# Two layers of a pooling, attention and product-key expert trunk on one core: pick transposes queued later, first V tiles by token tile, eight modulation rows moved from the U pass to the V pass

## The chip, the cores and the metric

The kernel runs on one core of one Trainium2 chip. The metric is the device time of one execution in microseconds (us). The time before is 1764.51 us, the median of three runs (1763.54 to 1767.49).

## What is computed

There are two layers, 256 tokens and 1024 channels. Each layer is a modulated norm, a mixer (causal pooling and sliding-window attention) and a PEER block, each with a gated residual. The modulation of a layer is six rows of 1024 values (`sh1, sc1, g1, sh2, sc2, g2`), a product of the conditioning vector with a 1024 x 6144 matrix. The change lies in the PEER block, cut here to what matters:

```python
mod = cond @ w_ada[l] + b_ada[l]                 # sh1, sc1, g1, sh2, sc2, g2
h2 = rms_norm(x, norm2_g[l]) * (1.0 + sc2) + sh2
q = (h2 @ wq).reshape(T, 8, 2, 128)
s = einsum('thpd,pnd->thpn', q, subkeys)         # 16 score rows of 128 keys for a token
top_s, top_i = top_k(s, 16)                      # then the 16 best sums of each head:
best_s, best_j = top_k(cand, 16)                 # 128 experts of 16384 for a token
gate = softmax(best_s)
act = gelu(h2 @ u[expert]) * gate
x = x + g2 * (act @ v[expert])
```

## The kernel before, in words

**Dense instead of gathered.** The kernel doesn't gather experts. It multiplies all 16384 rows of U and all of V, with a gate that is zero where an expert was not picked. The weights are 128 tiles of U and 128 of V a layer, each 128 x 1024 float32 (512 KB).

**The load stream.** One list of items (`Stream`, built at lines 199 to 218) holds every weight tile in the order of its use. SP issues the loads (L82) into a pool of five buffers called raw. A U or V tile is then split into two half-precision parts: ACT makes the high part (L87) and VectorE (DVE) the low part (L88), in one of five buffers called hl. Only when DVE has read it is a raw buffer free for the next load. Between the weight tiles, `spread` puts background items: rows of the modulation matrix (eight items of 512 KB for one of the six rows) and, in layer 0, the ten tiles of the next layer's input matrix ("pre"). A background row is consumed by one DVE instruction (L291, or L289 for the first of eight) that adds into one accumulator, acc_a; after the eighth, TensorE (PE) reduces it (L265 for scales and shifts, L302 for gains), and only then may the next row begin to fill acc_a.

**The U pass** (`peer`, the loop over `ip_`): 64 pairs of U tiles, 48 matmuls each (L362), then a gelu on ACT (L903) into act. While the first 32 pairs run, a generator `picks` (68 steps, `NPICK`) does the top-16 work on DVE, a fixed number of steps after each pair. Its last steps, for each token tile `tt` of 128 tokens, compare and add (L806 to L820), and end with four PE transposes (L829) and an ACT copy into pk (L830). From pair 32 on, a generator `gates` takes one step a pair: DVE builds one-hot tiles (L845 to L851), 16 small matmuls (L855, L857) make the gate of eight tokens for 64 of the 128 expert tiles, and DVE multiplies it into act (L860). A first round of 32 steps covers expert tiles 0 to 63 and ends with the U pass; a second round covers 64 to 127 and ends with V tile 63.

**The V pass**: for each pair of V tiles ACT (L929) and DVE (L930) split 512 columns of act (two expert tiles, 256 tokens each) into high and low parts in hbuf, which until then held the normed input that the U matmuls read. Each V tile is 12 matmuls of 512 columns (L370), six for each token tile. The last five tiles run token tile by token tile (`tail`), so that the residual of the first can start early.

**What sets the order.** Every engine works through a queue in a fixed order, which a scheduler writes at build time from the order in the program. `tc.issue_after(x)` only puts instructions behind x in the queue of x's own engine; it adds no wait between engines.

Of the kernel before, what the change touches and what calls it, by code (L numbers as in the profile page):

```python
# [121 lines left out]
def trunk(ctx, tc, ins, out):  # L122
# [82 lines left out]
    for l in range(L):  # L205
        if l == 1:
            items += conv_items(ins["wout"][1], 8, None, "pre")
        items += conv_items(ins["wq"][l], 16, WS, "w")
        uu = conv_items(ins["u"][l], 128, WS, "u")
        vv = conv_items(ins["v"][l], 128, VS, "v")  # L210
        if l == 0:
            uu = spread(uu, ada_rows(1, SC1) + ada_rows(1, SH1) + ada_rows(1, SC2), 8, 126)
            pre = conv_items(ins["win"][1], 10, None, "pre")
            vv = spread(vv, ada_rows(0, G2) + ada_rows(1, G1) + ada_rows(1, SH2) + pre, 66, 126)
        else:
            vv = spread(vv, ada_rows(1, G2), 66, 126)
        items += uu + vv
        vend[l] = len(items) - 1
# [137 lines left out]
    def mm_u(pt, w, hi, lo):  # L356

        wh, wl = (a.rearrange("p (k c) -> p k c", k=8) for a in w)
        n = 0
        for k in range(8):  # L360
            for a, b in ((wh, hi), (wh, lo), (wl, hi)):
                pe.matmul(pt, lhsT=a[:, k], rhs=b[:, k], start=n == 0, stop=n == 23)  # L362
                n += 1

    def mm_v(acc, w, ahi, alo, first, end):
# [356 lines left out]
    def peer(l, q5):  # L722
# [16 lines left out]
        def picks():  # L739

            If = [a.f(256, F16).rearrange("p (j r) -> p j r", j=16) for _ in range(2)]
            cand = a.f(8 * 112).rearrange("p (h m) -> p h m", h=8)
            B = a.f(256).rearrange("p (h r) -> p h r", h=16)
            J = a.f(256, U16).rearrange("p (h r) -> p h r", h=16)
            gt = a.f(256).rearrange("p (h r) -> p h r", h=16)
            m, t1, t2, ja = (a.f(256) for _ in range(4))
            jh = [a.f(512, F16).rearrange("p (n t) -> p n t", t=2) for _ in range(2)]
            o1 = a.f(2048, F16).rearrange("p (h r j) -> p h r j", h=8, r=16)
            o2 = a.f(2048, F16).rearrange("p (h r j) -> p h r j", h=8, r=16)
            ip = a.f(512, F16).rearrange("p (t s n) -> p t s n", t=2, s=2)  # L750
            gsum = a.f(16)
            gp = [a.f(256, F16) for _ in range(2)]
            Ji = a.f(256, I32)
            for j4 in range(4):
                for tt in range(2):
                    for j in range(j4 * 4, j4 * 4 + 4):
                        top16(V[tt][:, j], I[tt][:, j], sc[tt][:, j], tmp[j % 2])
                        yield
            V2 = [v.rearrange("p (h s) r -> p h s r", s=2) for v in V]
            I2 = [i.rearrange("p (h s) r -> p h s r", s=2) for i in If]  # L760
            for tt in range(2):
                dve.tensor_copy(If[tt], I[tt])
                for n, (alo, an, bn, c0) in enumerate(((0, 4, 16, 0), (4, 12, 4, 64))):
                    dve.tensor_tensor(
                        out=cand[:, :, c0:c0 + an * bn].rearrange("p h (a b) -> p h a b", a=an),
                        in0=V2[tt][:, :, 0, alo:alo + an].unsqueeze(3).to_broadcast([P, 8, an, bn]),
                        in1=V2[tt][:, :, 1, 0:bn].unsqueeze(2).to_broadcast([P, 8, an, bn]), op=ALU.add)
                yield
                for h in range(8):
                    top16(B[:, tt * 8 + h], J[:, tt * 8 + h], cand[:, h], tmp[h % 2][:, 0:112])  # L770
                    yield

            dve.tensor_tensor(out=gt, in0=B, in1=B[:, :, 0:1].to_broadcast([P, 16, 16]), op=ALU.subtract)
            yield

            dve.tensor_copy(Ji, J.rearrange("p h r -> p (h r)"))
            s4, s2 = m.bitcast(I32), ja.bitcast(I32)
            dve.tensor_scalar(s4, Ji, 4, None, op0=ALU.logical_shift_right)
            dve.tensor_scalar(s2, Ji, 2, None, op0=ALU.logical_shift_right)
            dve.tensor_scalar(t1, s4, 4.0, None, op0=ALU.is_ge)  # L780
            dve.scalar_tensor_tensor(t2, in0=s2, scalar=-12.0, in1=s4, op0=ALU.add, op1=ALU.subtract)
            dve.tensor_tensor(out=t2, in0=t2, in1=t1, op=ALU.mult)
            twice = [v.unsqueeze(2).to_broadcast([P, 256, 2]) for v in (t2, s4)]
            dve.tensor_tensor(out=jh[0], in0=twice[0], in1=twice[1], op=ALU.add)
            yield
            dve.tensor_scalar(s4, Ji, 15, None, op0=ALU.bitwise_and)
            dve.tensor_scalar(s2, Ji, 3, None, op0=ALU.bitwise_and)
            dve.tensor_tensor(out=t2, in0=s2, in1=s4, op=ALU.subtract)
            dve.tensor_tensor(out=t2, in0=t2, in1=t1, op=ALU.mult)
            dve.tensor_tensor(out=jh[1], in0=twice[0], in1=twice[1], op=ALU.add)  # L790
            yield

            def gate_split():
                dve.tensor_reduce(out=gsum, in_=gt, axis=AX.X, op=ALU.add)
                dve.reciprocal(gsum, gsum)
                dve.scalar_tensor_tensor(gt, in0=gt, scalar=GS,
                                         in1=gsum.unsqueeze(2).to_broadcast([P, 16, 16]),
                                         op0=ALU.mult, op1=ALU.mult)
                gf = gt.rearrange("p h r -> p (h r)")
                dve.tensor_copy(gp[0], gf)  # L800
                dve.tensor_tensor(out=gp[1], in0=gf, in1=gp[0], op=ALU.subtract)

            for tt in range(2):
                for s in range(2):
                    j4 = jh[s][:, tt * 128:tt * 128 + 128]
                    dve.tensor_tensor(out=o1.rearrange("p h r (c t) -> p (h r) c t", t=2),  # L806
                                      in0=j4.unsqueeze(2).to_broadcast([P, 128, 8, 2]),
                                      in1=iot16.rearrange("p (c t) -> p c t", t=2).unsqueeze(1).to_broadcast(
                                          [P, 128, 8, 2]),
                                      op=ALU.is_equal)  # L810
                    yield
                    if tt == 0 and s == 0:
                        act_e.activation(gt, gt, AF.Exp)
                    dve.tensor_tensor(out=o2, in0=o1,
                                      in1=I2[tt][:, :, s].unsqueeze(2).to_broadcast([P, 8, 16, 16]), op=ALU.mult)
                    yield
                    for w, (so, do) in ((8, (o2, o1)), (4, (o1, o2)), (2, (o2, o1))):
                        dve.tensor_tensor(out=do[:, :, :, 0:w], in0=so[:, :, :, 0:w], in1=so[:, :, :, w:2 * w],
                                          op=ALU.add)
                    dve.tensor_tensor(out=ip[:, tt, s].rearrange("p (h r) -> p h r", h=8), in0=o1[:, :, :, 0],  # L820
                                      in1=o1[:, :, :, 1], op=ALU.add)
                    yield
                if tt == 0:
                    gate_split()
                    yield
                pt = pg().bitcast(F16)
                ts = slice(tt * 128, tt * 128 + 128)
                for q, src in enumerate((ip[:, tt, 0], ip[:, tt, 1], gp[0][:, ts], gp[1][:, ts])):
                    pe.transpose(pt[:, q * 128:q * 128 + 128], src, id16)  # L829
                act_e.copy(pk[:, :, ts], pt[:, 0:512].rearrange("p (q t) -> p q t", q=4))  # L830
                yield

        NPICK = 32 + 2 * 9 + 4 + 2 * 7

# [60 lines left out]
        for ip_ in range(64):  # L895
# [6 lines left out]
                    key_scores(15)  # L902
            act_e.activation(act[:, ip_ * 512:(ip_ + 1) * 512], pt, AF.Gelu, scale=1.0 / WS)  # L903
            if ip_ < 32:
                while done < 10 + (NPICK - 10) * (ip_ + 1) // 31 and done < NPICK:
                    with tc.issue_after(st.hi_ins), tc.issue_after(st.lo_ins):
                        next(pick)
                    done += 1
            else:
# [8 lines left out]
        for i in range(128):  # L918
# [5 lines left out]
            if i % 2 == 0:  # L924
# [1 line left out]
                ahi = hb[:, slot * 1024:slot * 1024 + 512]  # L926
                alo = hb[:, slot * 1024 + 512:slot * 1024 + 1024]
                src = act[:, i * T:(i + 2) * T]
                tabs.append(act_e.activation(ahi, src, AF.Copy))  # L929
                dve.tensor_tensor(out=alo, in0=src, in1=ahi, op=ALU.subtract)  # L930
            st.limit = min(st.limit, vend[l])
            w = st.get("v")

# [1 line left out]
                s = slice(i % 2 * T + tt * 128, i % 2 * T + tt * 128 + 128)  # L935
                mm_v(accs[tt], w, ahi[:, s], alo[:, s], i == 0, i == 127)

            if i < 128 - NTAIL:
                mm(0)
                mm(1)  # L940
            else:
                tail.append(mm)
            if i < 64 and i % 2:
                next(gate)
        assert next(gate, 0) == 0 and next(pick, 0) == 0
# [97 lines left out]
```

## Time and profile before

| | us |
|---|---|
| median of three runs (1763.54 to 1767.49) | 1764.51 |
| the profiled execution | 1766.4 |
| its span, from the first to the last instruction | 1764.4 |
| PE busy in it | 1708.7 |
| DVE busy | 1397.7 |
| ACT busy | 857.7 |

The profiled execution is 1.9 us above the median of the runs, and 2.0 us of it lie outside the span. In the rows below, times are us from the span's start; the granted clock of PE is a share of 2.4 GHz, so that 0.50 is 1.2 GHz.

### The profile page before, as it was taken

Reading aid. Unit: us, or ns where it says so; the run is one execution under the profiler, and the core shown is the slowest. Engines: PE = TensorE matmul, PEld = TensorE weight load, DVE = VectorE, ACT = ScalarE, POOL = GpSimd, SP = SyncE. Lnnn points to the kernel's source line nnn. Section 1 sums busy time; section 2 is a strip of 40 time slices with the busy share of each in tenths; the row PEclk is TensorE's granted clock in tenths of the full one; section 3 lists DMA queues with packets and bytes.
Section 4 is the critical chain, followed back from the end, with each engine's and each line's share of the span. In section 5 each row is a group of like instructions: output and inputs, shape, how many; then the busy total and the mean of one; then the engine's idle time right before and its main releaser. Section 6 shows DMA issues by size and latency. Waiting matters only on the chain.

```text
span 1764.4 us, 33845 instructions
## 1 busy us (share of the span) xinstructions
PE 1708.7 (97%) x13652; PEld 1176.8 (67%) x13652; DVE 1397.7 (79%) x2576; ACT 857.7 (49%) x1164; POOL 9.4 (1%) x19
## 2 busy tenths in 40 slices
PE   6899999999999999999998999999999999999998
PEld 2448988989996544444455698888999845444443
DVE  3476799988889999878867578887888899986664
ACT  4355544544444444445656455454444444445553
POOL 0000000000000000000000000000000000000000
PEclk8999999999999999999999999999999999999999
DMA  8862677776775556678954066665555555556773
GB/s 333 324 242 97 194 238 252 225 225 208 223 217 189 184 190 206 228 259 319 312 173 142 18 198 197 204 203 181 181 190 181 185 182 184 190 186 214 228 228 123
DMA packets 100221, 364.02 MB, mean 206 GB/s; under 512 B 11713, under 2 KB 11729, under 8 KB 99681
## 3 DMA queue, kind: packets, MB, share of 16 engines
q1 hardware_dynamic: 99648, 361.29, 61.8%
q8 instruction: 106, 1.74, 0.4%
q0 software_dynamic: 416, 0.58, 0.1%
q14 instruction: 51, 0.41, 0.1%
HBM read 360.78 MB, written 1.05 MB: 205 GB/s over the span
## 4 chain that ended last, share of the span: by engine, by line
PE 88%; DVE 5%; DMA 3%; ACT 2%; issue 1%; SPq 0%; DVEq 0%; ACTq 0%
PE mm L362 40%; PE acc L370 37%; PE g L855 2%; PE g L857 2%; PE acc L362 2%; PE acc L496 1%; DVE hlt L88 1%; PE acc L325 1%; DMA rawt<-in_wq_dram 1%; DMA rawt<-in_adar_dram 1%; PE acc L876 1%; DVE act L88 1%; DMA hlt<-in_adar_dram 1%; ACT act L424 1%; PE mm L415 0%
## 5 line engine op out<-in xcount | busy, mean ns | idle before, releaser
L87 ACT ACTIVATE hlt<-rawt 128x1024 f16<-128x1024 f32 x544 | 571.6, 1052 | 408.9 <-PE acc L370 188.6
L88 DVE SCALAR_TENSOR_TENSOR hlt<-rawt,hlt 128x1024 f16<-128x1024 f32 x544 | 661.1, 1220 | 110.2 <-ACT hlt L87 104.9
L362 PE MATMUL mm<-hbuf,hlt 128*128 128x256 f16 x6672 | 745.2, 273 | 0.0
L362 PEld LDWEIGHTS <-hlt 128*128 128x128 f16 x7152 | 676.7, 98 | 81.5 <-issue 5.1
L370 PE MATMUL acc<-hlt,hbuf 128*128 128x512 f16 x3072 | 676.1, 380 | 6.6 <-ACT hbuf L929 6.5
L370 PEld LDWEIGHTS <-hbuf 128*128 128x128 f16 x3264 | 314.9, 98 | 380.8 <-issue 9.1
L903 ACT ACTIVATE act<-mm 128x512 f32<-128x512 f32 x128 | 76.4, 597 | 195.8 <-PE mm L362 195.8
L929 ACT ACTIVATE hbuf<-act 128x512 f16<-128x512 f32 x128 | 79.1, 627 | 103.4 <-PE acc L370 102.0
L930 DVE TENSOR_TENSOR hbuf<-act,hbuf 128x512 f16<-128x512 f32 x128 | 87.7, 689 | 32.3 <-ACT hbuf L929 32.3
L291 DVE SCALAR_TENSOR_TENSOR acc_a<-rawt,cond,acc_a 128x1024 f32<-128x1024 f32 x52 | 66.7, 1283 | 41.0 <-DMA rawt<-in_adar_dram 40.3
L845 DVE TENSOR_TENSOR lt<-iot,pk 128x1024 f16<-128x1024 f16 x128 | 87.6, 685 | 1.3 <-ACT pk L830 1.3
L860 DVE TENSOR_TENSOR act<-act,g 128x512 f32<-128x512 f32 x128 | 87.1, 681 | 1.5 <-PE g L857 1.5
L851 DVE TENSOR_TENSOR rl<-rt,pk 128x512 f16<-128x512 f16 x128 | 53.9, 421 | 32.2 <-PE g L857 31.6
L855 PE MATMUL g<-rl,lt 128*128 128x64 f16 x1024 | 78.3, 193 | 0.0
L857 PE MATMUL g<-rh,lt 128*128 128x64 f16 x1024 | 78.3, 193 | 0.0
L855 PEld LDWEIGHTS <-lt 128*128 128x128 f16 x1024 | 71.1, 97 | 8.0
L857 PEld LDWEIGHTS <-lt 128*128 128x128 f16 x1024 | 66.3, 97 | 8.0
L847 DVE TENSOR_TENSOR rt<-iot,pk 128x512 f16<-128x512 f16 x128 | 54.3, 424 | 3.8
L850 DVE TENSOR_TENSOR rh<-rt,pk 128x512 f16<-128x512 f16 x128 | 53.6, 419 | 0.0
L496 PEld LDWEIGHTS <-act 128*128 128x128 f16 x288 | 28.2, 101 | 30.6 <-DVE act L427 5.3
L370 PE MATMUL acc<-act,hbuf 128*128 128x512 f16 x192 | 45.9, 387 | 1.3 <-DVE act L376 1.3
L496 PE MATMUL acc<-act 128*128 128x512 f16 x192 | 45.8, 379 | 0.2 <-DVE act L88 0.2
(184 smaller groups left out, 862.0 us busy)
## 6 DMA issues: line engine op xcount, KB each, us to landing
rawt<-in_u_dram SPq DMA_DIRECT2D x256, 512.0 KB, 4.0
rawt<-in_v_dram SPq DMA_DIRECT2D x256, 512.0 KB, 4.0
rawt<-in_adar_dram SPq DMA_DIRECT2D x76, 512.0 KB, 4.6
rawt<-in_wq_dram SPq DMA_DIRECT2D x32, 512.0 KB, 4.6
hlt<-in_adar_dram SPq DMA_DIRECT2D x20, 512.0 KB, 9.9
rawt<-in_win_dram SPq DMA_DIRECT2D x20, 512.0 KB, 4.8
rawt<-in_wout_dram SPq DMA_DIRECT2D x16, 512.0 KB, 4.7
act<-in_msk_dram SPq DMA_DIRECT2D x2, 1024.0 KB, 7.4
```

Of the source, the lines that this page charges most:

```text
L87: self.hi_ins = self.nc.scalar.activation(hi, r, AF.Copy, scale=scale).ins
L88: self.lo_ins = self.nc.vector.scalar_tensor_tensor(lo, in0=r, scalar=scale, in1=hi, op0=ALU.mult, op1=ALU.subtract).ins
L362: pe.matmul(pt, lhsT=a[:, k], rhs=b[:, k], start=n == 0, stop=n == 23)
L370: last["mm"] = pe.matmul(acc[h], lhsT=a, rhs=b[:, h * 512:(h + 1) * 512], start=first and n == 0, stop=end and n == 2).ins
L496: pe.matmul(pt, lhsT=hm[:, b, k, tok[n]], rhs=w[:, cs], start=k + m == 0, stop=k == 7 and m == 2)
L845: dve.tensor_tensor(out=lt, in0=iot.unsqueeze(1).to_broadcast([P, 4, 128, 2]), in1=pv[0].to_broadcast([P, 4, 128, 2]), op=ALU.is_equal)
L855: pe.matmul(g3[:, t], lhsT=lt[:, t // 2, :, t % 2], rhs=rl[:, t // 2, :, t % 2], start=True, stop=False)
L857: pe.matmul(g3[:, t], lhsT=lt[:, t // 2, :, t % 2], rhs=rh[:, t // 2, :, t % 2], start=False, stop=True)
L860: dve.tensor_tensor(out=av, in0=av, in1=g3.rearrange("p t i -> p i t"), op=ALU.mult)
L903: act_e.activation(act[:, ip_ * 512:(ip_ + 1) * 512], pt, AF.Gelu, scale=1.0 / WS)
L929: tabs.append(act_e.activation(ahi, src, AF.Copy))
L930: dve.tensor_tensor(out=alo, in0=src, in1=ahi, op=ALU.subtract)
```

## The change

Four edits. In `picks`, the transposes become a function `turn(tt)`; `turn(0)` is called three steps later, inside the second token tile's work, and `turn(1)` remains the last step. The schedule of the steps is new: 67 of 68 steps are done by pair 29, none after pair 30, and `turn(1)` after pair 31 (before, all 68 were done by pair 30). The picks' PE instructions are also queued behind the last U matmul of their pair. In the V pass, the pair that begins each half (tiles 0 and 64) is split by token tile, and its matmuls run tile 0 first half, tile 1 first half, tile 0 second half, tile 1 second half. In layer 0, the eight items of layer 1's SC2 row leave the U pass (24 background items become 16) and join the V pass (34 become 42), between G1 and SH2.

```diff
         if l == 0:
-            uu = spread(uu, ada_rows(1, SC1) + ada_rows(1, SH1) + ada_rows(1, SC2), 8, 126)
+            uu = spread(uu, ada_rows(1, SC1) + ada_rows(1, SH1), 8, 126)
             pre = conv_items(ins["win"][1], 10, None, "pre")
-            vv = spread(vv, ada_rows(0, G2) + ada_rows(1, G1) + ada_rows(1, SH2) + pre, 66, 126)
+            vv = spread(vv, ada_rows(0, G2) + ada_rows(1, G1) + ada_rows(1, SC2) + ada_rows(1, SH2) + pre, 66, 126)
...
+            def turn(tt):
+
+                pt = pg().bitcast(F16)
+                ts = slice(tt * 128, tt * 128 + 128)
+                for q, src in enumerate((ip[:, tt, 0], ip[:, tt, 1], gp[0][:, ts], gp[1][:, ts])):
+                    pe.transpose(pt[:, q * 128:q * 128 + 128], src, id16)
+                act_e.copy(pk[:, :, ts], pt[:, 0:512].rearrange("p (q t) -> p q t", q=4))
...
+                    if tt == 1 and s == 0:
+                        turn(0)
+                        yield
                 if tt == 0:
                     gate_split()
                     yield
-                pt = pg().bitcast(F16)
...
-                yield
+            turn(1)
+            yield
...
-                while done < 10 + (NPICK - 10) * (ip_ + 1) // 31 and done < NPICK:
-                    with tc.issue_after(st.hi_ins), tc.issue_after(st.lo_ins):
+                while done < (NPICK if ip_ == 31 else min(NPICK - 1, 10 + (NPICK - 11) * (ip_ + 1) // 30)):
+                    with tc.issue_after(st.hi_ins), tc.issue_after(st.lo_ins), tc.issue_after(last["u"]):
                         next(pick)
...
-                tabs.append(act_e.activation(ahi, src, AF.Copy))
-                dve.tensor_tensor(out=alo, in0=src, in1=ahi, op=ALU.subtract)
+                for tt in range(2 if i % 64 == 0 else 1):
+                    h, lo, f = (v.rearrange("p (i t) -> p i t", t=T)[:, :, tt * 128:tt * 128 + 128]
+                                if i % 64 == 0 else v for v in (ahi, alo, src))
+                    tabs.append(act_e.activation(h, f, AF.Copy))
+                    dve.tensor_tensor(out=lo, in0=f, in1=h, op=ALU.subtract)
...
-            if i < 128 - NTAIL:
+            if i >= 128 - NTAIL:
+                tail.append(mm)
+            elif i % 64 == 0:
+                mm(0)
+                held_mm = mm
+            elif i % 64 == 1:
+                mm(0)
+                held_mm(1)
+                mm(1)
+            else:
                 mm(0)
                 mm(1)
-            else:
-                tail.append(mm)
```

## Rows read from the trace of the kernel before

**Rows 1.** The page's first part: busy us, share of the span and instructions of each engine.
```profile
PE 1708.7 (97%) x13652; PEld 1176.8 (67%) x13652; DVE 1397.7 (79%) x2576; ACT 857.7 (49%) x1164; POOL 9.4 (1%) x19
```
**Rows 2.** Busy time by stretch: length, busy us of PE, PEld, DVE, ACT and POOL (with instructions), granted PE clock, mean share of the DMA engines, GB/s. The stretches are the start; layer 0's picks, its V pass to tile 63 and two parts of the rest of that pass; and the second half of layer 1's V pass.
```profile
0.00:44.00 44.00, 26.66 (x146) 12.75 (x147) 14.56 (x37) 19.50 (x39) 3.98 (x11) 0.81 0.89 332
196.00:361.00 165.00, 162.63 (x1493) 145.72 (x1491) 154.48 (x432) 86.17 (x100) 0.00 (x0) 1.00 0.71 231
...
556.00:738.00 182.00, 179.73 (x1259) 89.55 (x1259) 166.62 (x254) 82.86 (x94) 0.00 (x0) 1.00 0.59 194
738.00:770.00 32.00, 31.71 (x140) 14.01 (x141) 24.12 (x25) 16.01 (x20) 0.00 (x0) 0.95 0.83 284
770.00:900.00 130.00, 130.00 (x604) 59.94 (x603) 101.46 (x100) 73.20 (x85) 2.87 (x4) 1.00 0.87 300
...
1600.00:1740.00 140.00, 140.00 (x650) 63.47 (x649) 92.38 (x89) 71.19 (x82) 0.00 (x0) 1.00 0.71 229
```
**Rows 3.** The waits of PE over the whole span: engine, output and line, what it waited for, us in total, times, the longest.
```profile
PE acc L370 <- ACT hbuf L929: 6.5, 4, 2.6
...
PE g L829 <- DVE act L820: 4.8, 2, 2.8
```
**Rows 4.** The timeline at the last picks of layer 0 (start, length, engine, line, operation; in brackets the idle time before and what ended it).
```profile
352.82 0.60 ACT L903 ACTIVATE act<-mm 128x512 f32<-128x512 f32 x1 [1.56 <-PE mm L362]
...
358.06 0.60 ACT L903 ACTIVATE act<-mm 128x512 f32<-128x512 f32 x1 [1.56 <-PE mm L362]
...
360.97 0.38 DVE L820 TENSOR_TENSOR act<-act 128x128 f16<-128x128 f16 x1
...
361.40 0.34 PE L829 MATMUL g<-id,act 128*128 128x128 f16 x3 [2.78 <-DVE act L820]
```
**Rows 5.** The same place in layer 1.
```profile
1216.82 0.50 PE L829 MATMUL g<-id,act 128*128 128x128 f16 x3 [2.04 <-DVE act L820]
```
**Rows 6.** The timeline from the U pass to the V pass of layer 0 (last gelu, last gate matmul, last gate multiplication, first V matmuls), and the first V matmuls of layer 1.
```profile
552.53 0.60 ACT L903 ACTIVATE act<-mm 128x512 f32<-128x512 f32 x1 [1.56 <-PE mm L362]
...
553.27 0.19 PE L857 MATMUL g<-rh,lt 128*128 128x64 f16 x1
553.33 0.68 DVE L860 TENSOR_TENSOR act<-act,g 128x512 f32<-128x512 f32 x1
...
554.73 10.72 PE L370 MATMUL acc<-hlt,hbuf 128*128 128x512 f16 x48 [1.26 <-ACT hbuf L929]
...
1408.62 2.73 PE L370 MATMUL acc<-hlt,hbuf 128*128 128x512 f16 x11 [1.26 <-ACT hbuf L929]
```
**Rows 7.** The timeline at V tile 64 of layer 0 and, in the last row, of layer 1.
```profile
735.54 0.19 PE L857 MATMUL g<-rh,lt 128*128 128x64 f16 x1
...
737.60 2.19 ACT L929 ACTIVATE hbuf<-act 128x512 f16<-128x512 f32 x4 [1.26 <-DVE act L860]
...
738.29 4.88 PE L370 MATMUL acc<-hlt,hbuf 128*128 128x512 f16 x14 [2.56 <-ACT hbuf L929]
...
1591.07 3.20 PE L370 MATMUL acc<-hlt,hbuf 128*128 128x512 f16 x14 [1.44 <-ACT hbuf L929]
```
**Rows 8.** Busy time by stretch, as in the second group: two stretches at the lower clock.
```profile
739.00:742.00 3.00, 3.00 (x9) 1.01 (x8) 3.00 (x5) 0.79 (x2) 0.00 (x0) 0.50 0.89 297
...
1217.00:1220.00 3.00, 3.00 (x17) 2.19 (x16) 0.90 (x1) 0.59 (x1) 0.00 (x0) 0.50 0.85 203
```
**Rows 9.** The page's groups of one line over the span (count, busy us, mean ns, idle before), and PE's reduction of an accumulated row in the stretch 541 to 545.
```profile
L929 ACT ACTIVATE hbuf<-act 128x512 f16<-128x512 f32 x128 | 79.1, 627 | 103.4 <-PE acc L370 102.0
L930 DVE TENSOR_TENSOR hbuf<-act,hbuf 128x512 f16<-128x512 f32 x128 | 87.7, 689 | 32.3 <-ACT hbuf L929 32.3
L291 DVE SCALAR_TENSOR_TENSOR acc_a<-rawt,cond,acc_a 128x1024 f32<-128x1024 f32 x52 | 66.7, 1283 | 41.0 <-DMA rawt<-in_adar_dram 40.3
...
L265 PE MATMUL g<-ones,acc_a 128*128 128x1 f32 x16 | 1.8, 245 | 0.0
```
**Rows 10.** The waits of SP's queue in the stretch 770 to 900.
```profile
SPq L82 <- DVE hlt L88: 59.9, 47, 2.4
...
SPq L82 <- DVE acc_a L291: 16.2, 15, 2.5
```
**Rows 11.** The waits of ACT's weight splits: two rows of the stretch 770 to 900, then one of the stretch 738 to 770.
```profile
ACT hlt L87 <- DMA rawt<-in_v_dram: 26.5, 17, 5.0
...
ACT hlt L87 <- PE acc L370: 6.7, 4, 2.0
...
ACT hlt L87 <- PE acc L370: 7.2, 5, 1.4
```
**Rows 12.** The timeline at the end of layer 0's V pass: the last matmuls, and the splits of the last V tiles.
```profile
888.65 22.39 PE L370 MATMUL acc<-hlt,hbuf 128*128 128x512 f16 x103
...
899.64 3.50 DVE L88 SCALAR_TENSOR_TENSOR hlt<-rawt,hlt 128x1024 f16<-128x1024 f32 x3 [0.87 <-ACT hlt L87]
```
**Rows 13.** The timeline where one background row ends and the next begins: SP's issues, then DVE's first addition of the next row.
```profile
781.38 3.01 SPq L82 DMA_DIRECT2D rawt<-in_v_dram  x2
788.27 0.33 SPq L82 DMA_DIRECT2D rawt<-in_adar_dram  x1
...
788.61 1.28 DVE L291 SCALAR_TENSOR_TENSOR acc_a<-rawt,cond,acc_a 128x1024 f32<-128x1024 f32 x1 [0.37 <-DMA acc_a<-in_brow_dram]
```
**Rows 14.** Busy time by stretch, as in the second group: the 60 us within 770 to 900 in which most was moved.
```profile
800.00:860.00 60.00, 60.00 (x284) 28.22 (x283) 48.52 (x48) 32.23 (x38) 0.72 (x1) 1.00 0.90 315
```

More of the change, by code (lines that the diff above doesn't have):

```diff
@@ L361, in mm_u @@
             for a, b in ((wh, hi), (wh, lo), (wl, hi)):
-                pe.matmul(pt, lhsT=a[:, k], rhs=b[:, k], start=n == 0, stop=n == 23)
+                last["u"] = pe.matmul(pt, lhsT=a[:, k], rhs=b[:, k], start=n == 0, stop=n == 23).ins
                 n += 1
@@ L825, in picks @@
                     yield
-                pt = pg().bitcast(F16)
[L827 to L830, printed above, removed]
-                yield
+            turn(1)
+            yield
         NPICK = 32 + 2 * 9 + 4 + 2 * 7
```

## The prediction

> **What bounds the kernel now.** I read the page's busy times first, then the stretches, then PE's own waits, and the timeline at each wait the change touches. PE is busy 97% of the span [rows 1], and in the PEER stretches it runs nearly without a gap: 130.00 of 130 us and 140.00 of 140 us in the two second halves of the V passes [rows 2]. Time can only come from PE's waits, from its clock, or from work taken off it. The change takes no work off it. Two groups of waits lie where it edits: 6.5 us in four places where V matmuls wait for L929, and 4.8 us in two places where the pick transposes wait for L820 [rows 3]. What a remedy might cost is seen in the loads. Layer 0's second V half moves 300 GB/s with the DMA engines 0.87 busy, the same half of layer 1 only 229 GB/s with 0.71 [rows 2].
>
> **Picks: 4.8 us.** In layer 0 the gelus start 5.24 us apart, the pace of a pair. PE finishes pair 30 at 358.0, and the transposes queued behind it start only when L820 has ended at 361.35: PE is idle for 2.78 us [rows 4]. In layer 1 it is 2.04 us [rows 5]. After the change the last DVE step belongs to pair 29 and its transposes stand behind pair 31, two pairs (10.5 us) later. L820 is now about 3.4 us late against pair 30. DVE has to do its pick steps one pair sooner; if it gained nothing at all on that, it would be 3.4 + 5.2 = 8.6 us late against pair 29, still within 10.5. It is 154.5 of 165 us busy there [rows 2], so it has little spare, but in layer 0 four of the rows' additions at 1.28 us [rows 9] leave this stretch (56 of the 118 steps over which 8 items were spread). So both waits go. The first token tile's transposes move three steps later. They land behind pair 28; the first gate is built behind pair 32, so nobody waits for them. The new ordering behind the last U matmul adds no wait, since the transposes wait there today.
>
> **V starts: 6.0 us.** Four waits: 1.26 and 1.26 us at tile 0 [rows 6], 2.56 and 1.44 us at tile 64 [rows 7]. All four wait for the last gate multiplication (L860), then for ACT. The change lets the twelve matmuls of the first token tile go first, 12 x 0.217 = 2.6 us (103 matmuls take 22.39 us [rows 12]). They need gates that were done 16 steps earlier. At tile 64 hbuf's first slot is long free, so the 2.56 and 1.44 us go wholly. At tile 0 hbuf is being read by the last U matmuls, and ACT first runs the gelu that ends at 553.13. Half a split I put at 0.35 us (half of the 0.63 us of L929 [rows 9], a little up), so it ends near 553.5, and PE's last gate matmul ends at 553.46 [rows 6]. I leave 0.25 us of wait there, and take 1.0 us at each. The bounds for these two are 0 (if ACT keeps a weight split ahead of the half) and 1.26 each. The second half of the split follows L860, which ends at 554.0, with 2.6 us of matmuls as its cover; without that cover it would be today's wait again. The one extra ACT and DVE instruction at each start cost some 0.35 us each of engines that are busy 82.9 and 166.6 of 182 us in the first V half [rows 2]; that idle time hides them, and without it they would cost 1.4 us of DVE time in all. The first V tile's weight buffer is held six matmuls longer, 1.3 us of one of five.
>
> **The clock: 3.1 us.** After two of these waits the granted clock is 0.50 (1.2 GHz): from 739 to 742, after the 2.56 us wait, and from 1217 to 1220, after the 2.04 us [rows 8]. After the 2.78 us wait it is not. The stretch 738 to 770 has a mean clock of 0.95 [rows 2], so 0.05 x 32 = 1.6 us lost, and three us at half clock are another 1.5. With the idle time in front of them gone, I take both back.
>
> **SC2's rows: minus 8.8 us.** The eight loads, their DVE additions and PE's 1.84 us of reduction [rows 9] leave layer 0's U pass, where PE doesn't wait for loads, and enter the second V half. PE's own work is the same in sum. But this half is where the stream is short. SP waits there for DVE to free raw buffers (59.9 us behind L88, 16.2 us behind L291 [rows 10]), and ACT's splits wait for landings 26.5 us and for PE only 6.7 us [rows 11]. It was ahead at the start: from 738 to 770 ACT waited 7.2 us for PE [rows 11]. By the end the lead is gone. The 103 matmuls that start at 888.65 end at 911.04; the last 36 of them begin with the last tile's first token tile, so at 911.04 - 36 x 0.217 = 903.2, and the last split ends at 903.14 [rows 12]. A load that comes later from here on is a wait of PE. What a load costs: 300 GB/s over 130 us are 74.4 loads of 0.524 MB, 1.75 us each [rows 2]; in the fullest 60 us that I read it is 315 GB/s [rows 14], 1.66 us. Eight loads at 1.66 are 13.3 us. Of that, PE's 1.8 us of reduction is covered, and the loads that fall in the first 32 of some 163 us, 1.6 of 8, use the spare time found there, 2.7 us. 13.3 - 1.8 - 2.7 = 8.8 us of new waits on PE. The bounds: nothing, if the stream can go at the 332 GB/s seen at the kernel's start [rows 2], since 102 loads, 53.5 MB, then take 161 us while PE works 60 x 2.6 + 4 x 1.8 = 163; and 8 x 1.75 - 1.8 = 12.2 if no spare time helps. I take 1.66 because it is from this very place.
>
> Here a rule pulls the other way. The Trainium skill (DMA: Bandwidth & Descriptors, Specifications) gives a core some 358 GB/s from memory as its limit. An estimate from it: 53.5 MB would take 149 us, less than PE's work, and the new waits would be none. By that the sum would be 8.8 us better. The trace disagrees for this place: SP waits there for buffers, and the fullest 60 us stay at 315 GB/s [rows 10, 14].
>
> **The sum.** -4.8 - 6.0 - 3.1 + 8.8 = -5.1 us. The profiled execution of 1766.4 (1764.4 of span and 2.0 outside) would become 1761.3. It lies 1.9 above the median of 1764.51, so the median would be 1759.4.
>
> **The rivals.**
> The stream keeps up. For it: 332 GB/s were moved at the start, and PE has no wait for a weight tile now. Against: the lead of zero at the end. Then -13.9: 1750.6. Chance 0.25.
> The loads take it all back, 11 to 15 us of waits, because a further change of row stands in the stream. For it: at such a change SP issued nothing from 784.4 to 788.27, since its buffer was held by a row that waited for acc_a [rows 13]. There will be four rows and so three changes in the place of two; a further 3.9 us on 8.8 gives 12.7, and the time would be 1763.3, no change that can be told. Chance 0.20.
> Slower. The same holes, with the lead gone before the first of them. Before, the lead hid them; if it is used up by the first change of row, each of three holes is a wait of 3.9 us: 12.2 + 11.7 = 23.9 against -13.9, so +10.0, 1774.5. Against: a hole is as long as DVE is ahead of PE, so it shrinks as the lead shrinks. It decides if the second V half of layer 0 grows by over 17 us. Chance 0.09.
> The change doesn't do what it says for the picks: DVE falls so far behind that the transposes wait at pair 31 too. Then 4.8 us and 1.5 us of clock stay: 1765.7. Against: the 8.6 of 10.5 us above. Chance 0.03.
> The forecast, with new waits of 4 to 11 us: 0.43.
>
> **The numbers.** A measurement of this kernel can tell about 0.2%, 3.5 us, from no change: 1761.0 and 1768.0 are the limits. The forecast's own range is 1754 to 1762, so some 0.05 of its 0.43 isn't a gain that can be told. Faster: 0.38 + 0.25 = 0.63. Same: 0.05 + 0.20 + 0.03 = 0.28. Slower: 0.09. The range goes from 1750, the stream keeping up, to 1765.5, which takes in nearly all that comes back through the loads, and leaves out the slower case.
>
> **What would show it.** Right: PE's list of waits has no row for L829 behind L820, and those behind L929 are under 1 us in sum; no stretch at 0.50 near 740 or 1217; in layer 0's V pass after tile 64 new waits of PE for L87 or L88, 5 to 10 us, and over 300 GB/s there; the U pass of layer 0 is shorter by 1.8 us more than the wait. Wrong: that V half with no PE wait (the price of a load was put too high) or with over 13 us (holes); PE waiting for L829 after pair 31; a new wait in the U pass behind a late weight split.

## The result, and the profile after

The changed kernel takes 1751.69 us (median of 5 runs, 1750.25 to 1755.88) against 1767.47 of the kernel before beside it (5 runs, 1763.54 to 1769.93): a ratio of 0.9926, 95% interval 0.991 to 0.9941. Run a second time, among the experiments, it gave 1751.6 us and 0.9915 (0.9896 to 0.9934). Its profiled execution is 1751.57 us with a span of 1749.8, 14.6 us under the span before. Faster was forecast, and 1751.69 lies in the range, but at its lower end. The likeliest case said 1759.4; what came out is the first rival, 1750.6, in which the stream of loads keeps up. The time lies in the range only because the range was drawn to take in this rival; the forecast's own bounds were 1754 to 1762.

PE's line of the page's first part, and then all that PE's list of waits has for the places of the change:

```profile
PE 1705.3 (97%) x13652; PEld 1174.0 (67%) x13652; DVE 1400.3 (80%) x2580; ACT 858.9 (49%) x1168; POOL 9.4 (1%) x19
```
```profile
PE acc L370 <- ACT hbuf L939: 0.5, 1, 0.5
```

The same 13652 instructions are busy 3.4 us less than in [rows 1], which is the clock (a net figure: from 78 to 86 us, where nothing was changed, this execution has a mean of 0.57 and the kernel before 0.79), and PE is idle 1749.8 - 1705.3 = 44.5 us in the place of 1764.4 - 1708.7 = 55.7, which is the waits: 11.2 us. 11.2 + 3.4 = 14.6. The prediction had 10.8 of waits and 3.1 of clock, before it took the 8.8 us for the loads off again. In the list, the 6.5 us behind L929 (now L939) have become 0.5, and the row of the pick transposes (4.8 us in [rows 3], now L808 behind L828) is gone.

The stretches of the changed kernel, with the columns of [rows 2]: layer 0's picks; two parts of its V pass after tile 64, and the fullest 60 us that were read; then the pick transposes of layer 1.

```profile
196.00:361.00 165.00, 165.00 (x1516) 147.75 (x1515) 149.71 (x425) 86.97 (x101) 0.00 (x0) 1.00 0.67 216
...
731.00:763.00 32.00, 31.48 (x146) 13.91 (x145) 27.27 (x29) 16.84 (x22) 0.00 (x0) 1.00 0.91 306
763.00:893.00 130.00, 130.00 (x613) 60.90 (x611) 109.01 (x107) 74.56 (x85) 2.87 (x4) 1.00 0.91 326
793.00:853.00 60.00, 60.00 (x283) 28.16 (x282) 51.26 (x53) 30.02 (x35) 0.00 (x0) 1.00 0.92 336
...
1205.00:1225.00 20.00, 20.00 (x211) 18.03 (x209) 14.10 (x21) 9.96 (x13) 0.00 (x0) 1.00 0.65 201
```

In the kernel before, a stretch at 0.50 (1.2 GHz) followed V tile 64 of layer 0, and another the pick transposes of layer 1 [rows 8]. Here tile 64 lies in the row from 731 and those transposes in the last row; both are at 1.00 (2.4 GHz). The row to look at is 763 to 893: with eight loads more in this half, PE is still busy for 130.00 of 130 us, and the rate is 326 GB/s where it was 300 [rows 2]. In the fullest 60 us it is 336, where it was 315 [rows 14] (320 from 795 to 855). No row of PE's list there is a wait for a weight tile.

The timeline of the changed kernel: the end of layer 0's picks, the start of its V pass, and tile 64.

```profile
358.65 0.39 DVE L828 TENSOR_TENSOR act<-act 128x128 f16<-128x128 f16 x1
...
361.74 0.39 PE L808 MATMUL g<-id,act 128*128 128x128 f16 x4
...
547.83 0.42 DVE L940 TENSOR_TENSOR hbuf<-act,hbuf 128x256 f16<-128x256 f32 x1
548.47 0.19 PE L864 MATMUL g<-rh,lt 128*128 128x64 f16 x1
548.50 1.24 PE L370 MATMUL acc<-hlt,hbuf 128*128 128x512 f16 x5
...
732.88 1.41 PE L370 MATMUL acc<-hlt,hbuf 128*128 128x512 f16 x5 [0.52 <-ACT hbuf L939]
```

The last pick addition ends at 359.04, 2.7 us ahead of its transposes, where it ended after PE was ready for them [rows 4]. At the V start the first half of the split is done at 548.25, ahead of PE's last gate matmul, and the V matmuls follow without a gap; the forecast had left 0.25 us there. At tile 64 one wait of 0.52 us is left, for the second half.

### The profile page after: what moved, and what is told of

Read it like the earlier page. It is cut to its first block, busy times and chain, and to the rows that moved or that the text cites. A ratio compares the mean times of both kernels' runs of the same rounds, so it can differ in the third digit from the quotient of the medians.

```text
span 1749.8 us, 33870 instructions
## 1 busy us (share of the span) xinstructions
PE 1705.3 (97%) x13652; PEld 1174.0 (67%) x13652; DVE 1400.3 (80%) x2580; ACT 858.9 (49%) x1168; POOL 9.4 (1%) x19
## 4 chain that ended last, share of the span: by engine, by line
PE 92%; DVE 3%; DMA 2%; ACT 2%; issue 1%; SPq 0%; DVEq 0%; ACTq 0%
PE mm L362 42%; PE acc L370 38%; PE g L862 2%; PE g L864 2%; PE acc L496 2%; PE acc L362 2%; PE acc L325 1%; DMA rawt<-in_adar_dram 1%; PE acc L883 1%; PE mm L496 1%; DMA hlt<-in_adar_dram 1%; DVE act L88 1%; ACT act L424 1%; DMA rawt<-in_wq_dram 1%; PE mm L415 0%
## 5 line engine op out<-in xcount | busy, mean ns | idle before, releaser
L939 ACT ACTIVATE hbuf<-act 128x512 f16<-128x512 f32 (+1 forms) x132 | 79.8, 613 | 97.4 <-PE acc L370 95.2
L940 DVE TENSOR_TENSOR hbuf<-act,hbuf 128x512 f16<-128x512 f32 (+1 forms) x132 | 88.2, 673 | 28.7 <-ACT hbuf L939 28.7
```

The source lines that it names most:

```text
L939: tabs.append(act_e.activation(h, f, AF.Copy))
L940: dve.tensor_tensor(out=lo, in0=f, in1=h, op=ALU.subtract)
```

## The experiments

Two theories stood. The **price** (the forecast): the stream was short before the change, so each further load is a wait of PE. The **keep-up** rival: the stream had spare capacity, and eight loads cost nothing. Beside them, each part of the change was to show its own worth. Each ratio is against the kernel before, run on the same chip.

**One part at a time.** e1_picks is the kernel before with `turn()`, the step schedule and the ordering behind the last U matmul; e2_vstart has only the change of the V loop; e3_sc2 only

```
-uu = spread(uu, ada_rows(1, SC1) + ada_rows(1, SH1) + ada_rows(1, SC2), 8, 126)
+uu = spread(uu, ada_rows(1, SC1) + ada_rows(1, SH1), 8, 126)
-vv = spread(vv, ada_rows(0, G2) + ada_rows(1, G1) + ada_rows(1, SH2) + pre, 66, 126)
+vv = spread(vv, ada_rows(0, G2) + ada_rows(1, G1) + ada_rows(1, SC2) + ada_rows(1, SH2) + pre, 66, 126)
```

and e4_no_sc2 is the changed kernel with those two lines as they were.

> Only the edit of the picks, the rest as before. If the waits of the transposes and the clock drop that follows the one of layer 1 are simply taken away: the 2.78 and 2.04 us are gone, the low clock near 1217 is gone (half of 3.4 us), so -6.5 us against before; the four waits for L929 stay at 6.5 us and the low clock near 739 stays. Rival, the wait is handed on: DVE is as late as before and the V pass waits longer for the last gate, so less than -3 us.

> Only the first V tiles of each half by token tile, the rest as before. If the waits are simply taken away: of 6.5 us at most 0.5 stay, and the low clock that follows the 2.56 us is gone (1.7 us), so -7.7 us. Rival, that low clock does not hang on that wait: -6.0 us and a stretch at 0.50 remains near 739. The transposes still wait 4.8 us.

> Only SC2's eight rows moved from layer 0's U pass to its V pass, the rest as before. By the price of a load that was read before (1.66 us each in the second V half, the lead at zero): PE waits of 5 to 11 us in that half, +9 us. By the rival, that the stream only went as fast as PE asked: no PE wait there, 320 GB/s or more in the 130 us after the first 32, and 0 to -2 us.

> The whole change but for SC2's rows, which stay in layer 0's U pass. If the move is neutral, the same time as the changed kernel (some 15 us under before, within 2 us of it) and 300 GB/s in the second V half. If the move is what lets DVE end the picks in time (4 additions of 1.28 us less before the last pick), the transposes of layer 0 wait here, 1 to 5 us, and layer 1 does not. By the price read before, 9 us faster than the changed kernel, which cannot be, since that one has no wait there.

| kernel | median us (runs) | ratio | at 1764.72 |
|---|---|---|---|
| e1_picks | 1756.51 (12) | 0.9958 (0.9944 to 0.9972) | -7.4 |
| e2_vstart | 1756.96 (11) | 0.9958 (0.9945 to 0.9972) | -7.4 |
| e3_sc2 | 1772.66 (7) | 1.0053 (1.0033 to 1.0073) | +9.4 |
| e4_no_sc2 | 1750.24 (6) | 0.9918 (0.9897 to 0.994) | -14.5 |

The last column is (ratio - 1) x 1764.72, the median of the kernel before in that comparison. PE's list of waits (columns as in [rows 3]) in e1_picks has this row at the places of the change, and none for the pick transposes:

```profile
PE acc L370 <- ACT hbuf L936: 7.8, 4, 3.8
```

That of e2_vstart has the row of L829 as it stands in [rows 3] and none for L929. That of e3_sc2 has both:

```profile
PE acc L370 <- ACT hbuf L929: 7.3, 4, 3.3
...
PE g L829 <- DVE act L820: 8.1, 2, 6.0
```

The first two kernels each lose the waits that they edit and keep the others (L936 in e1_picks is L929 before). Their gains add up to that of both: -7.4 - 7.4 = -14.8, measured -14.5 (by the intervals each of the two is known to some 2.5 us). The third looks like the price: 9.4 us slower (5.8 to 12.9), where 8.8 was forecast. It isn't. Its V half from 777 to 907 has PE busy throughout, at 318 GB/s, and 0.2 us of waits for weights in all; what has grown are the waits of the transposes, from 4.8 to 8.1 us, with a new one of 1.1 us for the first token tile's (L829 behind L801), and the clock behind them is low (stretches, columns of [rows 2]):

```profile
777.00:907.00 130.00, 130.00 (x612) 60.93 (x611) 108.55 (x107) 73.35 (x84) 2.87 (x4) 1.00 0.90 318
...
362.00:369.00 7.00, 4.59 (x25) 3.44 (x26) 3.51 (x6) 1.54 (x2) 0.00 (x0) 0.52 0.65 210
```

The timeline and DVE's waits say where the time goes. The last pick addition ends at 364.35 in the place of 361.35 [rows 4]. The first token tile's last one is late already, by 3.9 us, and that is before any tile of a gate is built (the first at 347.48). The kernel before, then e3_sc2:

```profile
336.38 0.38 DVE L820 TENSOR_TENSOR act<-act 128x128 f16<-128x128 f16 x1
```
```profile
340.24 0.38 DVE L820 TENSOR_TENSOR act<-act 128x128 f16<-128x128 f16 x1
...
363.96 0.39 DVE L820 TENSOR_TENSOR act<-act 128x128 f16<-128x128 f16 x1
364.41 0.50 PE L829 MATMUL g<-id,act 128*128 128x128 f16 x3 [6.05 <-DVE act L820]
```

From 196 to 340 DVE is busy 127.46 us in the place of 134.33, but it waits 17.5 us in the place of 8.7. Its main waits there, the kernel before first:

```profile
DVE hlt L88 <- ACT hlt L87: 5.2, 5, 2.6
DVE acc_a L291 <- DMA rawt<-in_adar_dram: 3.3, 5, 1.4
```
```profile
DVE acc_a L291 <- DMA rawt<-in_adar_dram: 8.7, 4, 2.8
DVE hlt L88 <- ACT hlt L87: 8.1, 6, 2.6
```

So taking DVE work out of the U pass made the last pick later: DVE runs a queue of fixed order, and ahead of the picks it stood longer in front of rows that had not landed and of splits that ACT had not made. Why these waits grew by more than the work fell was not tested. Neither theory had that. It is also what the pick schedule pays for in the whole change. Without SC2's move (e4_no_sc2) DVE waits 7.2 us from 196 to 340, and the last addition ends at 351.47, 10.6 us ahead of its transposes at 362.04; with it DVE waits 14.4 us there, and the lead is 2.7 us. The two-pair distance is large enough for both, so SC2's move costs nothing that these runs can tell, and gains nothing: 0.9918 without it, 0.9926 and 0.9915 with it, each inside the other's interval.

**Where the stream's limit is.** e5_after is the changed kernel again. e6_raw4 takes one of its five raw buffers away; e7_over50 and e8_over58 move one and two more rows into the V half (42 items become 50 and 58):

```
e6  -bufs=5
    +bufs=4        (the raw pool)
e7  +uu = spread(uu, ada_rows(1, SH1), 8, 126)
    +vv = spread(vv, ... SC2) + ada_rows(1, SH2) + ada_rows(1, SC1) + pre, 66, 126)
e8  +uu = spread(uu, [], 8, 126)
    +vv = spread(vv, ... SH2) + ada_rows(1, SC1) + ada_rows(1, SH1) + pre, 66, 126)
```

> The changed kernel again, on the chip of the three kernels that are measured with it. 0.992 to 0.993 of before; second V half of layer 0 at 326 to 336 GB/s without a wait of PE for a weight tile.

> The changed kernel with four raw buffers for loads in the place of five. If the five buffers set the rate of the stream (a buffer is held some 7.6 us from issue to release), a load takes 7.6 / 4 = 1.9 us, 102 loads 194 us against 163 us of PE work: PE waits some 25 us in the second V half of layer 0, at 275 GB/s. Rival, the DMA engines set it (0.91 busy there): a buffer less changes the rate by under 5% and PE waits under 5 us.

> The changed kernel with layer 1's SC1 row too in layer 0's V pass: 50 background items in the place of 42, 110 loads in 60 V tiles, 351 GB/s for PE not to wait. If a load has the price of 1.66 us that was predicted, eight of them less PE's 1.8 us of reduction: 11 us of new waits. If the stream went at PE's pace and has room up to 7.6 / 5 = 1.52 us a load (345 GB/s): 0 to 3 us.

> The same with SC1 and SH1, 58 background items, 118 loads, 372 GB/s for PE not to wait; no modulation row is left in the U pass. At 1.66 us a load: 23 us of new waits against the changed kernel. At 1.52 us a load: 179 us for 166 us of PE work, less the lead of 4 us, so 9 us. If PE waits under 3 us, the stream isn't at its end even there.

| kernel | median us (runs) | ratio | items |
|---|---|---|---|
| e5_after | 1751.6 (6) | 0.9915 (0.9896 to 0.9934) | 42 |
| e6_raw4 | 1774.93 (5) | 1.0049 (1.003 to 1.0068) | 42 |
| e7_over50 | 1764.25 (10) | 0.9985 (0.9971 to 0.9998) | 50 |
| e8_over58 | 1774.19 (5) | 1.0051 (1.0033 to 1.0068) | 58 |

The stretch from V tile 64 to the end of layer 0's V pass, in the kernel before, in e5_after, e6_raw4, e7_over50 and e8_over58, with the columns of [rows 2], a fence each:

```profile
738.30:911.00 172.70, 172.70 (x794) 79.05 (x795) 132.12 (x137) 92.36 (x111) 2.87 (x4) 0.99 0.85 291
```
```profile
729.50:905.10 175.60, 173.59 (x815) 80.33 (x812) 142.59 (x148) 94.59 (x113) 2.88 (x4) 1.00 0.88 310
```
```profile
735.10:932.30 197.20, 180.57 (x817) 81.12 (x814) 145.12 (x149) 94.91 (x113) 2.88 (x4) 0.98 0.82 278
```
```profile
727.40:911.70 184.30, 177.39 (x831) 81.55 (x827) 150.99 (x152) 94.06 (x110) 2.87 (x4) 1.00 0.89 318
```
```profile
725.10:919.40 194.30, 182.70 (x844) 83.54 (x840) 160.53 (x161) 95.34 (x110) 2.88 (x4) 0.99 0.90 323
```

Read the first and the last column of numbers together. The change with SC2's rows left where they were (34 items) was profiled twice, as e4_no_sc2 and as e9_no_sc2:

```profile
729.90:906.20 176.30, 173.63 (x800) 78.94 (x797) 134.58 (x140) 93.42 (x113) 2.87 (x4) 0.99 0.83 289
```
```profile
730.00:902.00 172.00, 171.35 (x801) 78.74 (x798) 133.80 (x140) 93.80 (x113) 2.88 (x4) 1.00 0.85 296
```

From 34 to 42 items the stretch doesn't grow by more than executions of one kernel differ: 176.3 and 172.0 us with 34, 175.6 and, in the first profile of the changed kernel, 173.6 with 42, PE's reduction of 1.84 us for the further row [rows 9] included; and the rate goes up. But e5_after didn't bring all that was expected of it. From 763 to 893 it moves 317 GB/s, where 326 to 336 stood, and PE waits 1.6 us for weights from 720 to 935; e4_no_sc2, with 34 items, has 2.1 us of such waits. So 42 items are near the edge.

```profile
763.00:893.00 130.00, 129.84 (x611) 60.84 (x610) 107.59 (x106) 73.67 (x84) 2.88 (x4) 1.00 0.90 317
```
```profile
PE acc L370 <- DVE hlt L88: 1.6, 3, 0.8
```

From 42 to 50 the stretch grows by 8.7, from 50 to 58 by 10.0, and its rate stays at 318 to 323. PE's waits for weights in the last two kernels, e7_over50 first:

```profile
PE acc L370 <- DVE hlt L88: 4.0, 10, 0.7
...
PE acc L370 <- ACT hlt L87: 1.1, 2, 0.7
```
```profile
PE acc L370 <- ACT hlt L87: 5.0, 7, 2.3
...
PE acc L370 <- DVE hlt L88: 4.6, 17, 0.6
```

These are the waits that the forecast had put one row too early: 5.1 us with 50 items, between the 0 to 3 and the 11 that were expected, and 9.6 with 58, close to the 9 that 1.52 us a load gave. With four buffers the rate falls to 278 GB/s with the same 42 items, PE waits 16.5 us for weights, and the stretch grows by 197.2 - 175.6 = 21.6 us: 25 us of waits were expected if the buffers set the limit. With four of them they do. With five it is open how far they do: 278 x 5 / 4 would be 347 GB/s, and e8_over58 gets 323 over its stretch, but 348 in the fullest 60 us that were read, where the DMA engines are 0.96 busy. No run has six buffers.

```profile
825.00:885.00 60.00, 58.37 (x289) 28.73 (x288) 52.17 (x53) 28.04 (x31) 1.44 (x2) 1.00 0.96 348
```

The span of e7_over50 is 1765.0 - 1752.0 = 13.0 us longer than that of e5_after. 8.7 of it lie in this stretch and 6.3 behind it, where PE waits 3.8 us for DVE (L415 behind L405) and the mean clock from 914 to 921 is 0.51; the part up to the V pass is 2.1 us shorter.

The Trainium skill (DMA: Bandwidth & Descriptors, Specifications) gives some 358 GB/s from memory as a core's limit. Its consequence, no new wait at 42 items, agrees with the runs (1.6 us of waits for weights in e5_after, 2.1 in e4_no_sc2). It doesn't tell where the waits begin: with 50 items PE asks for 349 GB/s, under that limit, and waits all the same, with 318 moved.

**The order in ACT's queue.** The last V tiles landed close before PE wanted them, and ACT waited there for tiles of `pre` while V tiles behind them had come. e10_pre_behind is e9_no_sc2 (e4's kernel again) with `pre` ordered behind the last V split:

```
+with tc.issue_after(st.hi_ins), tc.issue_after(st.lo_ins):
     take_pre(1)
```

> The change without the move of SC2's rows, again, beside the next kernel: 0.992 of before, two waits of PE of some 1 us each at the end of layer 0's V pass, ACT waiting some 16 us for the ten pre tiles there.

> The change without the move of SC2's rows, and the split of each pre tile queued behind the V splits that stand before it in the program. If the lost lead at the end of layer 0's V pass comes from ACT's queue (V splits behind a pre tile that has not landed): ACT waits under 6 us for pre tiles in the place of 16, PE has no wait of 0.9 us at the end, 1 to 4 us faster than without. Rival, the rate of the loads sets the lead: the same waits of PE, the same time.

ACT's waits for landings in e9_no_sc2 from 758 to 905, then those of e10_pre_behind, where the row of `pre` is missing and V tiles are waited for longer:

```profile
ACT hlt L87 <- DMA rawt<-in_v_dram: 33.2, 22, 5.2
ACT act L87 <- DMA rawt<-in_win_dram: 14.8, 10, 2.4
```
```profile
ACT hlt L87 <- DMA rawt<-in_v_dram: 41.0, 34, 4.4
```

The lead of tile 123, from the end of its split to its first matmul, grows from 2.5 to 6.5 us. In e4_no_sc2, the same kernel as e9_no_sc2, that split ended 0.3 us after PE could have begun, so executions differ by some 3 us here; 6.5 lies above both, which points to this order as what took the lead. The time doesn't follow: 1749.7 us (6 runs), 0.9914 (0.9897 to 0.993), against 1750.01 (6 runs), 0.9916 (0.9902 to 0.993), since PE had a wait of only 0.65 us there, where two of some 1 us were expected. The stretch from tile 64 is 171.1 us long in the place of 172.0.

**The two halves of the pick edit.** e11_old_steps is the changed kernel with the step schedule of before; e12_turn0_early has the new schedule, with `turn(0)` where it was, behind `gate_split()`:

```
e11 -while done < (NPICK if ip_ == 31 else min(NPICK - 1, 10 + (NPICK - 11) * (ip_ + 1) // 30)):
    +while done < 10 + (NPICK - 10) * (ip_ + 1) // 31 and done < NPICK:
e12 -if tt == 1 and s == 0:
    -    turn(0)
    -    yield
     if tt == 0:
         gate_split()
         yield
    +    turn(0)
    +    yield
```

> The changed kernel with the old schedule of pick steps (all 68 done by pair 30), turn(0) late as in the change. If the distance of two pairs between the last DVE step and its transposes is what removes the wait: the transposes stand behind pair 30 and wait 2 to 4 us in layer 0, a low clock may follow, +2 to +5 us against the changed kernel. Rival, moving turn(0) is enough, since DVE then builds no gate tiles ahead of the last pick: no wait, the same time.

> The changed kernel with turn(0) at its old place, right after the first token tile, and the new schedule. If only the distance matters: no wait for the transposes, the same time. Rival, DVE puts the first gates' tiles (some 4 us of work) ahead of the last pick again, and the margin of 2.7 us that the changed kernel has in layer 0 is used up: the transposes wait 1 to 3 us there, and none in layer 1.

e11_old_steps takes 1760.98 us (10 runs), 0.9976 (0.9965 to 0.9988); e12_turn0_early 1760.14 (8 runs), 0.9966 (0.9949 to 0.9983). PE's waits in the first and in the second:

```profile
PE g L808 <- DVE act L828: 7.2, 2, 5.9
```
```profile
PE g L808 <- DVE act L800: 5.0, 1, 5.0
PE g L808 <- DVE act L801: 1.1, 1, 1.1
```

Without the new schedule the last transposes wait, as in e3_sc2, and longer than was expected (5.9 us in layer 0, where 2 to 4 stood). With it, but with `turn(0)` early, the last ones don't, and the first token tile's do: the schedule runs ahead of DVE, and PE meets them before `gate_split()` (L800, L801) has ended. That was in neither expectation. Leaving out either half gives back 0.9966 or 0.9976 against 0.9915 to 0.9926, some 7 to 11 us of 1765.

The ordering behind the last U matmul has no run of its own: with `tc.issue_after(last["u"])` left out of the changed kernel, every engine has the same instructions in the same order, so that part does nothing by itself. No version here beats the changed kernel beyond the intervals.

## Why the prediction was right, and where it was wrong

**Picks, -4.8: right in size, partly wrong in its reason.** Both waits are gone [rows 3, 4, 5]. "Within 10.5 us" held, but the help that was seen in four additions leaving this stretch was none: SC2's move alone made the last pick 3.0 us later (e3_sc2), and in the whole change it took 10.6 - 2.7 = 7.9 us of lead. DVE did have less to do there, 149.71 us in the place of 154.48 [rows 2], but from 196 to 340 it waited 14.4 us in the place of 8.7.

**V starts, -6.0: right.** 6.5 us became 0.5. The wait that is left is at tile 64 and not at tile 0, where ACT had the half split done ahead of PE's last gate matmul.

**The clock, -3.1: right.** PE is busy 3.4 us less, net of the low clock near 80 us, and at both places of [rows 8] the clock is at 1.00.

**SC2's rows, +8.8: the step that failed.** The eight loads cost 0 to 2 us and not 8.8 (1751.69 and 1751.6 us with them, 1750.24 and 1750.01 without), for three reasons that the runs show.
- The step took 1.66 to 1.75 us a load as what the stream can do [rows 2, 14]. That was what PE asked for: by the prediction's terms, 60 x 2.6 us and three reductions of 1.84 for 60 + 34 loads are 161.5 / 94 = 1.72 us a load, 305 GB/s, and 300 were moved. With 42 items it asks for 163.4 / 102 = 1.60 us, 327 GB/s, and 326 are moved (317 in e5_after). With 50 it asks for 165.2 / 110 = 1.50 us, 349 GB/s; there the whole stretch from tile 64 gets 318, hardly more than the 310 to 314 with 42, and PE waits. A rate that is read while nobody waits is a demand, not a limit.
- "By the end the lead is gone" rested on the last split, which ends at 903.14 for matmuls at 903.2 [rows 12]. That holds only for the last five tiles, whose first token tiles PE takes all in a row, 1.3 us each in the place of 2.6, so that it meets the last tile early. Tile 123, the first of the five, tells more. Its split in the kernel before is this row:

```profile
893.22 1.22 DVE L88 SCALAR_TENSOR_TENSOR hlt<-rawt,hlt 128x1024 f16<-128x1024 f32 x1
```

  It ends at 894.44, and the tile's first matmul stands 60 matmuls ahead of the end, at 911.04 - 60 x 0.217 = 898.0: a lead of 3.6 us. In the changed kernel the same two events are

```profile
879.75 23.47 PE L370 MATMUL acc<-hlt,hbuf 128*128 128x512 f16 x108
883.29 1.22 DVE L88 SCALAR_TENSOR_TENSOR hlt<-rawt,hlt 128x1024 f16<-128x1024 f32 x1
```

  and the lead is 903.22 - 60 x 0.217 - 884.51 = 5.7 us. In e5_after, the same kernel, it is 2.0, and in e3_sc2, with as many loads, 3.7: the lead differs by that much from one execution to the next, and the eight loads didn't end it.
- Part of the missing lead was, as far as these runs show, ACT's order and not the stream: in the kernel before ACT waited for `pre` tiles (first row, 770 to 900), in the changed one hardly (second, 763 to 893), and e10_pre_behind took this wait away and had a lead of 6.5 us.

```profile
ACT act L87 <- DMA rawt<-in_win_dram: 15.6, 10, 2.5
```
```profile
ACT act L87 <- DMA rawt<-in_win_dram: 2.5, 5, 0.7
```

Where the stream is short, the price itself was a third too high by these two kernels: eight loads more lengthen the stretch by 10.0 us (e8_over58 against e7_over50), PE's reduction included, where the forecast's 8 x 1.66 are 13.3. The larger error is where it begins: behind 42 items and not at 34.

**The holes at a change of row** (second and third rival) are there, three of them, and none became a wait of PE. SP's issues of the changed kernel around the first:

```profile
762.15 3.31 SPq L82 DMA_DIRECT2D rawt<-in_v_dram  x2
769.31 0.33 SPq L82 DMA_DIRECT2D rawt<-in_adar_dram  x1
```

It lasts 769.31 - 765.46 = 3.85 us; the others, up to 796.73 and 830.41, last 2.89 and 2.18. The first came near: tile 85 behind it was split only 1.6 us ahead of its first matmul, the smallest lead in this half ahead of the last five tiles. Whether a hole shrinks with the lead, the argument against the slower case, three holes don't tell.

What stays open is what bounds the stream with five buffers, and why DVE waits longer when SC2's additions leave the U pass. Also, the low clock that follows a wait isn't told by the wait's length (below), so the 3.1 us could be read off the rows, and not worked out for another kernel.

## What to carry to other kernels

A rate in a trace in which nobody waits is a demand: work out what the bounding engine asks for per load, and only where less than that arrives is it the stream's limit; then move one unit more at a time until waits appear. A lead is read ahead of the tail, not at the last tile, where the consumer runs at another pace, and in more than one execution. Taking work off an engine that runs an interleaved order can make the step that counts later, as here, where the engine then waited longer ahead of that step; parts that cost 9 us alone can cost nothing where another part gives them distance, so each part is tried alone and left out.

## What the runs showed of the hardware

- The length of a wait of PE doesn't tell whether its clock falls. After 2.78 us in the kernel before [rows 4] it stayed at 1.00 (first row); after 2.80 us at the same place of e2_vstart it fell to 0.50 (second), and after 2.04 us too [rows 5, 8]:

```profile
361.40:364.40 3.00, 3.00 (x29) 2.72 (x30) 1.84 (x3) 1.13 (x2) 0.00 (x0) 1.00 0.69 240
```
```profile
362.50:365.50 3.00, 2.96 (x16) 2.22 (x17) 1.88 (x3) 0.59 (x1) 0.00 (x0) 0.50 0.67 227
```

- The longest waits were followed by the longest stretches at the low clock. With 6.05 us (e3_sc2, up to 364.41) the mean is 0.52 from 362 to 369, and with 5.86 us (e11_old_steps, up to 362.06) 0.53 from 360.5 to 367, so the clock was down before the wait had ended. With 5.02 us (e12_turn0_early, up to 339.31) the mean is 0.52 from 339 to 342.5 (row below) and 0.76 up to 346, and after 2.04 and 2.56 us three us at 0.50 were seen [rows 8]:

```profile
339.00:342.50 3.50, 3.19 (x17) 2.33 (x18) 3.47 (x6) 0.59 (x1) 0.00 (x0) 0.52 0.92 300
```

- The stream of 0.524 MB loads went at 336 GB/s for 60 us with five buffers and 42 items, and at 348 with 58, the DMA engines 0.92 and 0.96 busy. With four buffers it went at 278 over the whole second half of the V pass, where five gave 310 in the same comparison.
